# The input products of the feed-forwards as seven half-block products instead of eight

## The chip, the cores and the metric

The kernel runs on one core of a Trainium2 chip. The metric is the device time of one execution in microseconds (us). TensorE is called PE (its weight loads PEld), VectorE DVE, ScalarE ACT, GpSimd POOL; SP is the engine that issues most transfers. PSUM is the memory that PE writes.

## The reference, cut to what matters

Two transformer blocks in a row on 512 tokens of width D = 1024, all in float32. Three feed-forwards take part: two in the first block (before and after a mixer), one at the end of the second.

```python
def swiglu_ffn(h, w_in, w_out):              # DFF = 2816
    a, b = jnp.split(h @ w_in, 2, axis=-1)
    return (jax.nn.silu(a) * b) @ w_out

x = x + 0.5 * swiglu_ffn(rmsnorm(x, ffn1_norm_g), ffn1_w_in, ffn1_w_out)
...
x = x + 0.5 * swiglu_ffn(rmsnorm(x, ffn2_norm_g), ffn2_w_in, ffn2_w_out)
...
x = x + _swiglu(_rms(x, norm_ffn_w[l]), w_ffn_gate[l], w_ffn_up[l], w_ffn_down[l])
```

Between them stand the mixers (sparse attention, convolution, attention to a memory; then sliding-window attention and gated linear attention; then attention to a second memory), which the change leaves as they are.

## The kernel before, in words

Activations lie transposed: `X` is eight tiles of 128 features x 512 tokens. Every float32 operand of a product is split into a high part rounded to the matmul's type (a cast on ACT) and a low part (the rest, a subtraction on DVE or POOL); `mm3` (line 229) makes three matmuls of a product: high x high, high x low, low x high. `split` (258) does it for one tile.

`ffn` (513) works on 22 units c in three groups of 8, 7 and 7 (`FGROUPS`). A unit's weights are two tiles of 128 x 1024, one for the gate columns and one for the up columns, `f1_ab[2c]` and `[2c+1]`. `w` (272) loads one (`wr`, on SP) and splits it (`wh`, `wl`). `chunk` (302) multiplies it with the eight tiles `xh`, `xl` of the normalised X: 24 matmuls of 512 columns into one PSUM tile, so 48 for a unit. The row scale `rb` of the normalisation is applied after the product: z = gate * rb, Silu, * rb, u = z * up, and u is split. After the units of a group come its output products: eight chunks, one for each tile of X, each over the group's 8 or 7 u tiles, added to X. In the first unit (c = 0) the product walks over k for both tiles together, so that it can start before the last tile of X is normalised. `lag` (2 in the first feed-forward, else 1) says after which unit the row scale `rc`, `rb` is made; until then products wait in PSUM. The third feed-forward ends in `tail` (569), whose last four output tiles are made in halves of 256 columns.

`hook(n)` is called as each X tile is final; it begins the next stage's normalisation: `norm_x` (389) multiplies by the gain and splits (`xs`), `norm_sq` (378) sums squares (on POOL for the first stage). `project` (1249) is the last product of a mixer and calls it; so does the output loop of `xattn` (1662). In the first feed-forward, `tick` (507) lets small steps of other work in: the position tables (`tables`, 473: DMAs on POOL, a few matmuls) and the preparation of the memory (`mem_prep`, 643). The weights' low parts are made on DVE in the feed-forwards, and two thirds of them on POOL in the mixers (`wes`).

A scheduler lays the instructions on each engine's queue in advance, by program order as their inputs come ready; at run time each queue goes in that order. PSUM has eight tiles of 512: tags g (3), s (2), t (2), o (1); `psf` (222) goes round the first seven.

Of the kernel before, what the change touches and what calls it, by code (L numbers as in the profile page):

```python
# [14 lines left out]
P = 128  # L15
# [14 lines left out]
LINEW = 64  # L30

# [169 lines left out]
class _Net:  # L201
# [24 lines left out]
    def mm(self, o, l, r, first, last):  # L226
        self.pm = self.nc.tensor.matmul(o, l, r, start=first, stop=last)  # L227

    def mm3(self, o, lh, ll, rh, rl, first, last):
        self.mm(o, lh, rh, first, False)  # L230
        self.mm(o, lh, rl, False, False)
        self.mm(o, ll, rh, False, last)
# [22 lines left out]
    def copy(self, o, x):  # L255
        self.nc.scalar.copy(o, x)  # L256
# [116 lines left out]
    def begin_norm(self, key=None):  # L373
        self.nk = key
        self.acc = self.t(self.g, [P, S], F32, "acc", 1)
        self.xh, self.xl = [], []
# [12 lines left out]
    def norm_x(self, j):  # L389

        if self.nk:
            h = self.t(self.g, [P, S], F32R, "xs", 16)
            l = self.t(self.g, [P, S], F32R, "xs", 16)
            gc = self.cc(self.nk, j)
            self.last = self.nc.scalar.activation(h, self.X[j], AF.Copy, scale=gc)
            self.stt(l, self.X[j], gc, h.bitcast(F32), ALU.mult, ALU.subtract)
            self.xh.append(h)
            self.xl.append(l)
# [27 lines left out]
    def setup(self):  # L426
# [13 lines left out]
        for j in range(KT):  # L440
            nc.sync.dma_start(self.X[j], a["xT"][j])
            if j < 4:
                ws[j % 2][j // 2]()
# [29 lines left out]
    def tables(self, p):  # L473

        nc, a = self.nc, self.a
        box = {}

        def line(key, width, n):
            def go():
                if "rel" not in box:  # L480
                    box["rel"] = self.t(p, [33, 16], F32, "rel", 1)
                    nc.vector.memset(box["rel"], 1.0)
                    nc.gpsimd.dma_start(box["rel"][0:32], a["rel"])
                oh = self.load(key, pool=p)
                box[key] = self.t(p, [16, 2 * width], F32, key + "l", 1)
                for j in range(2):
                    ps = self.ps("t", (16, width))
                    s = slice(width * j, width * (j + 1))
                    self.mm(ps, box["rel"], oh[:, s], True, True)
                    nc.vector.tensor_copy(box[key][:, s], ps)  # L490
# [8 lines left out]
        def cmpline():  # L499
            nc.gpsimd.dma_start(self.drel, box["oh1"])  # L500
            nc.gpsimd.dma_start(self.dcmp, box["oh2"])

        st = [line("oh1", LINE // 2, 2), line("oh2", 512, 2), cmpline]
# [9 lines left out]
    def ffn(self, key, scale, hook, lag=1):  # L513
        nc = self.nc
        with self.pool(key) as p:
            self.wps = [self.wps[0], (p, D, 2)]
            for gi, (k0, k1) in enumerate(FGROUPS):
                uh, ul = [], []
                wait = []
                for c in range(k0, k1):  # L520
                    pa, pb = self.psf(), self.psf()
                    if c == 0:

                        ws = [self.w(key + "_ab", u, D) for u in range(2)]
                        for k in range(KT):
                            s = slice(k * P, (k + 1) * P)
                            for ps, (h, l) in zip((pa, pb), ws):
                                self.mm3(ps, h[:, s], l[:, s], self.xh[k], self.xl[k], k == 0, k == KT - 1)
                    else:
                        self.chunk(pa, key + "_ab", 2 * c, self.xh, self.xl)  # L530
                        if c == lag:
                            with self.tc.issue_after(self.pm.ins):
                                self.rc
                        self.chunk(pb, key + "_ab", 2 * c + 1, self.xh, self.xl)
                    if c == lag:
                        with self.tc.issue_after(self.pm.ins):
                            self.rb
                    wait.append((pa, pb))
                    if c < lag:
                        continue  # L540
                    for pa, pb in wait:
                        z = self.t(p, [P, S], F32, "z", 3)
                        self.mul(z, pa, self.rb)
                        self.act(z, z, AF.Silu)
                        self.mul(z, z, self.rb)
                        u = self.t(p, [P, S], F32, "u", 2)
                        self.mul(u, z, pb)
                        h = self.t(p, [P, S], F32R, "uh", 8)
                        l = self.t(p, [P, S], F32R, "ul", 8)
                        self.split(h, l, u)  # L550
                        uh.append(h)
                        ul.append(l)
                        self.tick()
                    wait = []
                last = gi == len(FGROUPS) - 1
                if last and hook is None:
                    self.tail(p, f"{key}_o{gi}", uh, ul)
                    break
                for n in range(KT):
# [4 lines left out]
                    if last:  # L564
                        hook(n)
# [1222 lines left out]
```

## Time and profile before

| | us |
|---|---|
| median of 3 runs (2480.50 to 2482.72) | 2481.11 |
| profiled execution | 2480.74 |
| its span | 2478.7 |
| PE busy | 2406.0 (97%) |
| DVE, ACT, POOL busy | 1433.1, 980.3, 407.7 |

The span runs from the first to the last instruction. The first feed-forward lies at about 7 to 380 us, the second at 1158 to 1518, the third at 2100 to the end. Matmuls overlap, so their pace is read from the distance of their starts, not from the duration of one.

### The profile page before, as it was taken

Reading aid. Unit: us, or ns where it says so; the run is one execution under the profiler, and the core shown is the slowest. Engines: PE = TensorE matmul, PEld = TensorE weight load, DVE = VectorE, ACT = ScalarE, POOL = GpSimd, SP = SyncE. Lnnn points to the kernel's source line nnn. Section 1 sums busy time; section 2 is a strip of 40 time slices with the busy share of each in tenths; the row PEclk is TensorE's granted clock in tenths of the full one; section 3 lists DMA queues with packets and bytes.
Section 4 is the critical chain, followed back from the end, with each engine's and each line's share of the span. In section 5 each row is a group of like instructions: output and inputs, shape, how many; then the busy total and the mean of one; then the engine's idle time right before and its main releaser. Section 6 shows DMA issues by size and latency. Waiting matters only on the chain.

```text
span 2478.7 us, 30104 instructions
## 1 busy us (share of the span) xinstructions
PE 2406.0 (97%) x11566; PEld 1990.4 (80%) x11566; DVE 1433.1 (58%) x2594; ACT 980.3 (40%) x1743; POOL 407.7 (16%) x223
## 2 busy tenths in 40 slices
PE   9999999999999999999999999999999998999998
PEld 6888888787777887778888888787788886888887
DVE  7444455864777666775534444558765277644444
ACT  4222234343444544453322233544565256322222
POOL 5000004231222232231000002121212430000000
PEclk9999999999999999999999999999999999999999
DMA  5622325221222121124232322121212242322321
GB/s 196 187 93 96 99 88 172 96 101 54 78 69 76 53 87 69 65 87 134 95 101 86 108 87 98 59 94 54 68 69 76 99 145 68 124 94 92 104 80 49
DMA packets 84051, 232.26 MB, mean 94 GB/s; under 512 B 16305, under 2 KB 25457, under 8 KB 83908
## 3 DMA queue, kind: packets, MB, share of 16 engines
q1 hardware_dynamic: 75460, 224.87, 27.3%
q0 software_dynamic: 8448, 5.48, 0.7%
q8 instruction: 91, 1.49, 0.2%
q14 instruction: 52, 0.43, 0.1%
HBM read 223.85 MB, written 11.64 MB: 95 GB/s over the span
## 4 chain that ended last, share of the span: by engine, by line
PE 47%; DVE 5%; ACT 1%; issue 1%; POOL 0%; DVEq 0%; ACTq 0%; POOLq 0%
PE g L227 24%; PE s L227 11%; PE t L227 10%; PE o L227 1%; PE t L235 1%; DVE q L238 0%; DVE sp L1523 0%; DVE wl L238 0%; DVE xs L250 0%; DVE og L238 0%; DVE ptl L238 0%; ACT wh L256 0%; DVE og L250 0%; DVE x L238 0%; DVE stl L238 0%
## 5 line engine op out<-in xcount | busy, mean ns | idle before, releaser
L227 PE MATMUL g<-xs,wh 128*128 128x512 f32 x2800 | 892.2, 396 | 1.3 <-DVE kcr L238 1.0
L256 ACT CAST wh<-wr 128x1024 fp32r<-128x1024 f32 (+6 forms) x405 | 411.5, 1017 | 1046.9 <-PE g L227 400.4
L227 PEld LDWEIGHTS g<-xs,wh 128*128 128x128 f32 x2800 | 523.1, 190 | 106.3 <-issue 4.1
L227 PE MATMUL g<-xs,wl 128*128 128x512 f32 x1400 | 553.2, 395 | 1.5 <-DVE wl L238 1.5
L238 POOL TENSOR_TENSOR wl<-wr,wh 128x1024 fp32r<-128x1024 f32 (+6 forms) x134 | 309.9, 2314 | 1415.7 <-ACT wh L256 1366.7
L238 DVE TENSOR_TENSOR wl<-wr,wh 128x1024 fp32r<-128x1024 f32 (+4 forms) x271 | 335.5, 1240 | 78.4 <-ACT wh L256 72.6
L227 PEld LDWEIGHTS g<-xs,wl 128*128 128x128 f32 x1400 | 265.3, 190 | 59.3 <-issue 3.1
L227 PE MATMUL t<-xs,wh 128*128 128x512 f32 x672 | 208.8, 392 | 2.1 <-ACT xs L256 1.9
L227 PE MATMUL s<-xs,wh 128*128 128x512 f32 x672 | 208.2, 390 | 2.0 <-ACT wh L256 1.8
L227 PEld LDWEIGHTS s<-xs,wh 128*128 128x128 f32 x672 | 126.1, 188 | 31.9 <-ACT wh L256 3.4
L227 PEld LDWEIGHTS t<-xs,wh 128*128 128x128 f32 x672 | 126.6, 189 | 29.1 <-ACT xs L256 2.3
L227 PE MATMUL t<-xs,wl 128*128 128x512 f32 x336 | 131.6, 392 | 0.3 <-DVE wl L238 0.3
L227 PE MATMUL s<-xs,wl 128*128 128x512 f32 x336 | 130.9, 390 | 0.0
L253 ACT ACTIVATE sp<-sp,nm 128x128 f32<-128x128 f32 x192 | 101.9, 532 | 48.9 <-DVE nm L1071 37.8
L238 DVE TENSOR_TENSOR ptl<-t,pth 128x512 fp32r<-128x512 f32 (+1 forms) x128 | 72.9, 603 | 56.8 <-ACT pth L256 56.5
L256 ACT CAST pth<-t 128x512 fp32r<-128x512 f32 (+1 forms) x128 | 61.7, 520 | 98.4 <-PE t L235 98.2
L227 PE MATMUL g<-uh,wh 128*128 128x512 f32 (+1 forms) x242 | 92.1, 380 | 0.0
L227 PE MATMUL g<-uh,wl 128*128 128x512 f32 (+1 forms) x242 | 92.0, 380 | 0.0
L227 PE MATMUL g<-ul,wh 128*128 128x512 f32 (+1 forms) x242 | 92.0, 380 | 0.0
L227 PEld LDWEIGHTS t<-xs,wl 128*128 128x128 f32 x336 | 63.5, 189 | 14.1 <-DVE wl L238 0.8
L227 PEld LDWEIGHTS s<-xs,wl 128*128 128x128 f32 x336 | 63.1, 188 | 12.9
L238 POOL TENSOR_TENSOR y<-y,rmb 128x512 f32<-128x512 f32 x2 | 3.6, 1786 | 402.8 <-ACT rmb L256 402.8
(468 smaller groups left out, 3947.8 us busy)
## 6 DMA issues: line engine op xcount, KB each, us to landing
wr<-f_ab SPq DMA_DIRECT2D x130, 512.0 KB, 3.5
wr<-f_o SPq DMA_DIRECT2D x48, 448.0 KB, 3.2
wr<-m_f SPq DMA_DIRECT2D x40, 512.0 KB, 3.2
wr<-m_o SPq DMA_DIRECT2D x40, 512.0 KB, 3.4
wr<-f_o SPq DMA_DIRECT2D x24, 512.0 KB, 3.6
wr<-m_q SPq DMA_DIRECT2D x12, 512.0 KB, 3.5
dline<-drel POOLq DMA_DIRECT2D x8, 640.0 KB, 20.1
wr<-m_km SPq DMA_DIRECT2D x8, 512.0 KB, 3.6
```

The costliest lines, as they stand in the source:

```text
L227: self.pm = self.nc.tensor.matmul(o, l, r, start=first, stop=last)
L235: self.nc.tensor.transpose(o, i, self.ident)
L238: (e or self.nc.vector).tensor_tensor(o, x, y, op=op)
L253: return self.nc.scalar.activation(o, x, f, **k)
L256: self.nc.scalar.copy(o, x)
```

## The change

A unit's product is seen as blocks. Rows: gate, up. Inner dimension: the first and the second half of the 1024 features. Columns: the first and the second 256 tokens (H = 256). With a11, a12 the halves of the gate weights and a21, a22 those of the up weights, and likewise x1 and x2 (tiles 0 to 3 and 4 to 7 of X) cut into lo and hi, the four result blocks come from seven block products and sums (Winograd's form of Strassen's algorithm). A block product is 4 k-tiles x 3 matmuls of 256 columns. For each unit `wforms` makes four sums of weight halves on POOL and seven splits; for each feed-forward `form_x` makes, in place of `norm_x`, the four sums of X halves for each pair of tiles (n, n+4) and splits all seven 256-column blocks (`bh`, `bl`). Tiles of X are taken in the order 0, 4, 1, 5, 2, 6, 3, 7. The first two units of the first feed-forward stay plain. A unit's last block (a22) is put behind the first block of the next unit. The memory's preparation moves into the last group of the first feed-forward; the steps of `tables` each take their own tiles and issue their own transfer.

```diff
+    def form_x(self, n):
+        i = n % 4
+        xg = self.t(self.tp, [P, S], F32, "xg", 3)
+        self.last = self.act(xg, self.X[n], AF.Copy, scale=self.cc(self.nk, n))
+        self.half_x[n] = xg
+        if self.B[i] is None:
+            self.B[i] = [self.t(self.fp, [P, 64 + 7 * H], F32R, k, 4)[:, 48:48 + 7 * H] for k in ("bh", "bl")]
+        bh, bl = self.B[i]
+        def parts(c, x):
+            n = x.shape[-1]
+            self.last = self.copy(bh[:, c:c + n], x)
+            self.tt(bl[:, c:c + n], x, bh[:, c:c + n].bitcast(F32), ALU.subtract)
+        if n < 4:
+            parts(0, xg[:, :H])
+        else:
+            parts(H, xg)
+        if i in self.half_x and i + 4 in self.half_x:
+            x1, x2 = self.half_x[i], self.half_x[i + 4]
+            t = self.t(self.tp, [P, 4 * H], F32, "xt", 1)
+            t1, t2, t3, t4 = (t[:, k * H:(k + 1) * H] for k in range(4))
+            self.tt(t1, x1[:, H:], x1[:, :H], ALU.subtract)
+            self.tt(t2, x2[:, H:], t1, ALU.subtract)
+            self.tt(t3, x2[:, H:], x1[:, H:], ALU.subtract)
+            self.tt(t4, x2[:, :H], t2, ALU.subtract)
+            parts(3 * H, t)
...
+    def wforms(self, arr, c):
...
+        (a11, a12), (a21, a22) = ((r[:, :B], r[:, B:]) for r in raw)
+        s1, s2, s4, s3 = (self.t(self.fw, [P, B], F32, "ws", 4) for _ in range(4))
+        e = nc.gpsimd
+        self.tt(s1, a21, a22, ALU.add, e)
+        self.tt(s2, s1, a11, ALU.subtract, e)
+        self.tt(s4, a12, s2, ALU.subtract, e)
+        self.tt(s3, a11, a21, ALU.subtract, e)
...
+            for m, (k, x) in enumerate(pair):
+                out[k] = h[:, m * B:m * B + B], l[:, m * B:m * B + B]
+                self.split(*out[k], x)
...
+        def first():
+            box["w"] = self.wforms(key + "_ab", c)
+            box["r1"] = self.psf(half)
+            self.block(box["r1"], box["w"]["a11"], 0, True)
+        def second():
+            w = box["w"]
+            e1 = box["e1"] = self.t(p, [P, H], F32, "e1", 2)
+            self.copy(e1, box["r1"])
+            r5 = box["r5"] = self.psf(half)
+            self.block(r5, w["s1"], 3, True)
+            e5 = box["e5"] = self.t(p, [P, H], F32, "e5", 2)
+            self.copy(e5, r5)
+        def rest():
...
+            self.block(r2, w["s2"], 4, True)
+            self.block(r1, w["a12"], 1)
+            self.tt(r2, r2, e1, ALU.add)
+            self.copy(e2, r2)
+            self.block(r5, w["s4"], 2)
+            self.block(r2, w["s3"], 5)
+        def last():
+            e3 = box["e3"] = self.t(p, [P, H], F32, "e3", 2)
+            self.copy(e3, box["r2"])
+            self.block(box["r2"], box["w"]["a22"], 6)
+        def act(uh, ul):
+            e = nc.gpsimd
+            lo, hi = slice(0, H), slice(H, S)
+            z = self.t(p, [P, S], F32, "z", 2)
+            self.mul(z[:, lo], box["r1"], self.rb[:, lo])
+            self.tt(z[:, hi], box["r5"], box["e2"], ALU.add)
+            self.mul(z[:, hi], z[:, hi], self.rb[:, hi], e)
+            self.act(z, z, AF.Silu)
+            self.mul(z, z, self.rb, e)
+            c22 = box["e5"]
+            self.tt(c22, c22, box["e3"], ALU.add, e)
+            u = self.t(p, [P, S], F32, "u", 1)
+            self.mul(u[:, lo], z[:, lo], box["r2"])
+            self.mul(u[:, hi], z[:, hi], c22, e)
+            self.keep_u(u, uh, ul)
...
+            for c in range(n + 1):
...
+                if c < np_:
+                    waiting.append(self.plain(p, key, c, *parts[gi]))
+                    continue
+                if c < n:
+                    first, second, rest, end, act = self.unit(p, key, c)
+                    first()
...
+                if prev:
+                    prev[0]()
+                if c < n:
+                    second()
...
+                if prev:
+                    waiting.append(prev[1])
+                if c >= lag:
+                    flush()
+                if c and gi != group[c - 1]:
+                    products(group[c - 1])
+                if c < n:
+                    rest()
+                    prev = end, lambda act=act, gi=gi: act(*parts[gi])
...
-                    self.norm_x(n)
+                    (self.form_x if key.startswith("ffn") else self.norm_x)(n)
```

## Rows read from the trace of the kernel before

**Rows 1.** The page: busy us by engine, share of the span, instructions.
```profile
PE 2406.0 (97%) x11566; PEld 1990.4 (80%) x11566; DVE 1433.1 (58%) x2594; ACT 980.3 (40%) x1743; POOL 407.7 (16%) x223
```

**Rows 2.** Chain of waits in the second feed-forward: start us, us, what.
```profile
1186.73 5.44 PE s L227 x24
```

**Rows 3.** Busy time of the engines by stretch.
```profile
core 0: us, PE busy (x) PEld busy (x) DVE busy (x) ACT busy (x) POOL busy (x), PEclk, DMA share, GB/s
12.00:30.00 18.00, 17.42 (x74) 13.22 (x73) 17.96 (x11) 8.33 (x11) 17.84 (x11) 1.00 0.78 269
1168.00:1246.00 78.00, 78.00 (x354) 64.85 (x353) 39.36 (x58) 25.47 (x33) 0.00 (x0) 1.00 0.31 101
1246.00:1284.00 38.00, 38.00 (x169) 31.50 (x168) 14.01 (x15) 7.89 (x8) 0.00 (x0) 1.00 0.30 97
```

**Rows 4.** PE in order of time, output products in halves, third feed-forward.
```profile
2443.31 0.28 PE L227 MATMUL t<-uh,wh 128*128 128x256 f32 x1
...
2445.82 0.28 PE L227 MATMUL g<-uh,wh 128*128 128x256 f32 x1
```

**Rows 5.** Groups by form: xcount, busy us, mean ns (second: tile kr, min/median/max ns).
```profile
L238 DVE TENSOR_TENSOR ul<-u,uh 128x512 fp32r<-128x512 f32 x66 | 44.9, 683 | 0.0
L238 DVE TENSOR_TENSOR kr<-g,rmb x8: 401/424/426, 383.5 to 402.8; 128x256 f32<-128x256 f32 x8
...
L256 ACT CAST wh<-wr 128x1024 fp32r<-128x1024 f32 x327 | 343.4, 1052 | 826.9 <-PE g L227 312.8 <-issue 260.4 <-PE s L227 128.4
L253 ACT ACTIVATE z<-z 128x512 f32<-128x512 f32 x66 | 41.1, 627 | 0.9 <-DVE z L238 0.8
L256 ACT CAST uh<-u 128x512 fp32r<-128x512 f32 x66 | 40.5, 616 | 2.9 <-DVE u L238 2.9
L395 ACT ACTIVATE xs<-x,cols 128x512 fp32r<-128x512 f32 x48 | 33.1, 718 | 17.4 <-DVE x L250 14.0 <-DVE x L238 2.5 <-DMA cols<-cols 0.8
L256 ACT CAST pth<-t 128x256 fp32r<-128x256 f32 x32 | 11.6, 364 | 0.0
...
L238 POOL TENSOR_TENSOR x<-x,ga 128x512 f32<-128x512 f32 x8 | 10.3, 1288 | 31.8 <-DVE ga L250 31.8
L496 POOL DMA_DIRECT2D dline<-drel x8 | 8.6, 1071 | 35.4 <-issue 33.7 <-DMA drel<-oh1l 1.7
L238 POOL TENSOR_TENSOR wl<-wr,wh 128x256 fp32r<-128x256 f32 x1 | 0.8, 772 | 3.4 <-DMA wr<-cw 3.4
```

**Rows 6.** DVE and POOL in order of time: start us, us, instruction.
```profile
10.18 1.23 DVE L250 SCALAR_TENSOR_TENSOR xs<-x,cols,xs 128x512 fp32r<-128x512 f32 x1 [0.48 <-ACT xs L395]
10.82 1.74 POOL L238 TENSOR_TENSOR wl<-wr,wh 128x512 fp32r<-128x512 f32 x1
11.51 1.60 DVE L250 SCALAR_TENSOR_TENSOR xs<-x,cols,xs 128x512 fp32r<-128x512 f32 x1
...
17.82 12.72 DVE L238 TENSOR_TENSOR wl<-wr,wh 128x1024 fp32r<-128x1024 f32 x6
```

**Rows 7.** PE in order of time, first feed-forward: unit 2 begins; row scale.
```profile
30.75 0.61 PE L227 MATMUL s<-xs,wh 128*128 128x512 f32 x2
...
37.73 0.27 PE L227 MATMUL o<-ones,acc 128*128 128x2 f32 x1 [1.39 <-POOL acc L238]
```

**Rows 8.** In order of time, start of the second feed-forward.
```profile
1157.52 0.62 PE L227 MATMUL g<-xs,wh 128*128 128x512 f32 x2
...
1158.24 0.68 DVE L250 SCALAR_TENSOR_TENSOR x<-t,x 128x512 f32<-128x512 f32 x1
```

**Rows 9.** In order of time, start of the third feed-forward.
```profile
2095.75 0.69 DVE L238 TENSOR_TENSOR x<-s,x 128x512 f32<-128x512 f32 x1 [1.02 <-PE s L227]
...
2097.55 0.74 DVE L250 SCALAR_TENSOR_TENSOR xs<-x,cols,xs 128x512 fp32r<-128x512 f32 x1
...
2100.31 0.39 PE L227 MATMUL g<-xs,wh 128*128 128x512 f32 x1
...
2103.92 1.22 DVE L238 TENSOR_TENSOR wl<-wr,wh 128x1024 fp32r<-128x1024 f32 x1
```

More of the change, by code (lines that the diff above doesn't have):

```diff
@@ L224, in psf, with mm, mm3 @@
         return self.ps("gsgtgst"[self.pi], shape)
[L226 to L232, printed above, removed]
+    def mm(self, o, l, r, first, last, more=False):
+        self.pm = self.nc.tensor.matmul(o, l, r, start=first, stop=last, skip_group_check=more)
+    def mm3(self, o, lh, ll, rh, rl, first, last, more=False):
+        self.mm(o, lh, rh, first, False, more)
+        self.mm(o, lh, rl, False, False, more)
+        self.mm(o, ll, rh, False, last, more)
     def tr(self, o, i):
@@ L255, in copy @@
     def copy(self, o, x):
-        self.nc.scalar.copy(o, x)
+        return self.nc.scalar.copy(o, x)
     def split(self, h, l, x):
@@ L439, in setup @@
         ws = [self.w("f1_ab", u, D, split=True) for u in range(2)]
-        for j in range(KT):
+        for n, j in enumerate(ORDER):
             nc.sync.dma_start(self.X[j], a["xT"][j])
-            if j < 4:
-                ws[j % 2][j // 2]()
+            if n < 4:
+                ws[n % 2][n // 2]()
         for u in range(2):
@@ new lines, in block, with unit @@
+    def block(self, ps, w, b, first=False):
+        h, l = w
+        c = slice(b * H, b * H + H)
+        for i in range(4):
+            s = slice(i * P, i * P + P)
+            bh, bl = self.B[i]
+            self.mm3(ps, h[:, s], l[:, s], bh[:, c], bl[:, c], first and i == 0, i == 3, not first)
+    def unit(self, p, key, c):
+        nc = self.nc
+        box = {}
+        half = (P, H)
+        def first():
[11 more added lines that the diff above has]
+        def rest():
+            w, r1, r5, e1 = (box[k] for k in ("w", "r1", "r5", "e1"))
+            e2 = box["e2"] = self.t(p, [P, H], F32, "e2", 2)
+            r2 = box["r2"] = self.psf(half)
+            self.block(r2, w["s2"], 4, True)
[23 more added lines that the diff above has]
+            self.keep_u(u, uh, ul)
+        return first, second, rest, last, act
@@ new lines, in keep_u, with plain, act @@
+    def keep_u(self, u, uh, ul):
+        h = self.t(self.up, [P, S], F32R, "xs", 16)
+        l = self.t(self.up, [P, S], F32R, "xs", 16)
+        self.split(h, l, u)
+        uh.append(h)
+        ul.append(l)
+        self.tick()
+    def plain(self, p, key, c, uh, ul):
+        pa, pb = self.psf(), self.psf()
+        if c == 0:
+            ws = [self.w(key + "_ab", u, D) for u in range(2)]
+            for k in ORDER:
+                s = slice(k * P, (k + 1) * P)
+                for ps, (h, l) in zip((pa, pb), ws):
+                    self.mm3(ps, h[:, s], l[:, s], self.xh[k], self.xl[k], k == 0, k == KT - 1)
+        else:
+            self.chunk(pa, key + "_ab", 2 * c, self.xh, self.xl)
+            self.chunk(pb, key + "_ab", 2 * c + 1, self.xh, self.xl)
+        def act():
+            z = self.t(p, [P, S], F32, "z", 2)
+            self.mul(z, pa, self.rb)
+            self.act(z, z, AF.Silu)
+            self.mul(z, z, self.rb)
+            u = self.t(p, [P, S], F32, "u", 1)
+            self.mul(u, z, pb)
+            self.keep_u(u, uh, ul)
+        return act
@@ L515, in ffn @@
+    def ffn(self, key, scale, hook, np_=0, lag=1, after=None):
         with self.pool(key) as p:
             self.wps = [self.wps[0], (p, D, 2)]
[L517 to L554, printed above, removed]
@@ L555, in ffn, with flush, products @@
+            self.fw = p
+            parts = [([], []) for _ in FGROUPS]
+            group = [gi for gi, (k0, k1) in enumerate(FGROUPS) for _ in range(k0, k1)]
+            waiting = []
+            def flush():
+                while waiting:
+                    waiting.pop(0)()
+            prev = None
+            def products(gi):
+                k0, k1 = FGROUPS[gi]
+                uh, ul = parts[gi]
                 last = gi == len(FGROUPS) - 1
+                if last:
+                    after()
@@ L556, in ffn @@
                 if last and hook is None:
                     self.tail(p, f"{key}_o{gi}", uh, ul)
-                    break
-                for n in range(KT):
+                    return
+                for n in ORDER:
                     po = self.psf()
@@ L1259, in project @@
         hook = self.hook
-        for n in range(KT):
+        for n in ORDER:
             po = self.psf()
@@ L1712, in step, with after @@
                 return hook
+            fin = None
+            def after():
+                self.fpool.__exit__(None, None, None)
+                if self.fpool is not fin:
+                    self.open_x()
             def done(tag):
```

155 lines of the change are left out of this document (109 added, 46 removed).

## The prediction

> **What bounds the kernel now.** I read the page first: TensorE (PE) is busy for 97% of the span [rows 1]. That number hides which stages have slack, so next comes the chain of waits inside the second feed-forward: it is PE alone, 5.44 us for each run of 24 matmuls, a run on the heels of the other; one of them stands in [rows 2]. The table of stretches shows it at the full clock (1.00), and room on the others: in the 78 us of input products DVE works 39 us, ACT 25 us, POOL nothing; in the 38 us of output products DVE works 14 us [rows 3]. So a feed-forward is bound by the count and pace of matmuls, and 50% of DVE and all of POOL stand free. The profiled execution took 2480.74 us, against a median of 2481.11; the sum below is made against 2480.7.
>
> **What the change removes.** A unit (one block of 128 gate and 128 up columns) has 48 matmuls of 512 columns now: two runs of 24, 10.88 us [rows 2]. It becomes 84 matmuls of 256 columns. The kernel already has such a stream, in its last output products: from 2443.31 to 2445.82 twenty-one of them start, 0.120 us apart [rows 4], against 0.227 us for 512 (5.44/24). Half the columns cost 53%, not 50%, so seven eighths of the work costs 84 x 0.120 = 10.08 us: 0.80 us less a unit. Two units of the first feed-forward stay plain; 64 units change: **-51 us**. The Trainium skill ("TensorE: Matmul & The Clock Gate", Back-to-back issue gap) gives N/2.4 + 2.5 ns, an estimate of 109 and 216 ns; by that a unit would lose 1.2 us and the whole 76 us. The rows are this kernel's own operand type, so they decide.
>
> **What it adds per unit.** ACT: seven casts of 512 at 0.62, four copies of 256 from PSUM at 0.36, Silu and the cast of u: 7.0 us. DVE: seven low-part subtractions and that of u, 8 x 0.68, and four operations of 256 with a PSUM operand at 0.42: 7.1 us. POOL: four weight sums and one product of 512 at 1.29, three operations of 256 at 0.77: 8.8 us [rows 5]. Each alone fits under 10.08 us.
>
> DVE and POOL do not add up that way. At 10.18 us a DVE subtraction and a POOL one meet: POOL starts at 10.82 and ends 1.15 us after the DVE one (11.41 to 12.56), and the next DVE one, begun at 11.51, ends 0.55 us after POOL's (13.11) [rows 6]; alone they take 1.29 and 0.74 [rows 5, 9]. So an operation of DVE with two SBUF operands and one of POOL take turns, 1.70 us a pair of 512. From 12 to 30 us both read as 99% busy [rows 3], and six of DVE's 1024-wide splits take 12.72 us, 2.1 each instead of 1.22 [rows 6]: each mostly waits for the other. In turns, a unit needs POOL 5 x 1.15 + 3 x 0.63 (0.77 less the same 0.14) and DVE 8 x 0.55: **12.0 us** of the shared path, more than PE's 10.08. The operations with one PSUM operand are not counted: the eight of 256 at 383 to 403 us, where POOL splits weights too, spread from 0.40 to 0.43 us only [rows 5]. The Trainium skill ("SBUF — State Buffer", Who interferes with whom) speaks against this change: the shared port pair is an exclusive lock, and the second to issue fully blocks until the first finishes. By whole durations that would be 8.8 + 5.4 = 14.2 us a unit; the trace agrees on the turns, but shows 1.70 us for a pair where whole durations give 1.97.
>
> What softens it is the output products. In those 38 to 43 us DVE has 14 us of work and POOL none [rows 3], so the next unit's four sums (4.6 us) and its first two splits (1.1) can be done ahead; the single set of four sum tiles and five split buffers allow no more. Between two such stretches PE has seven units, 70.6 us, and some 4 us more before the last u tile is read (18 matmuls at 0.227). The shared path needs 7 x 12.0 less what is done ahead and what the next stretch takes over (three sums, five splits: 6.2), about 72 us. That fits, just. The first eight units have no such stretch before them: 8 x 12.0, less unit 0's sums (4.6) and with unit 8's first sum and splits (2.3), 94 us against 83.5 of PE (eight units, two blocks of the ninth) and the same 4. So the stall lies between nothing (PE's bound) and 64 x 1.96 = 125 us (turns without any catching up). I take 6.5 us for each first group and 2 us for the hand-offs in each of the others, 33 us for three feed-forwards with f1's shorter first group counted alike: units of 10.6 us on average. What is late next is DVE: behind a subtraction that waits for POOL stands the addition of e1 to r2, for which ACT's copy e2 waits and PE's block s3 with it; two blocks (2.9 us) cover it, so it breaks only where two POOL operations fall into that time. In the same way the copy e3 is covered by the next unit's first block (1.44 us).
>
> **The starts.** The forms cost DVE, per pair of X tiles, a subtraction of 256, one of 512, four differences of 256 and a subtraction of 1024: 0.42 + 0.68 + 1.68 + 1.22 = 4.0 us, against two of 0.74 for the plain split [rows 9], and nearly all of them must be there before the second block of the first unit.
> - f1: PE leaves the two plain units at 30.75 us and so far waits first near 36 us, 1.39 us for POOL's sum of squares [rows 7]; DVE and POOL have no free time before [rows 3]. DVE is rid of four of the six splits [rows 6] and gets 16 us of forms. They begin in earnest when the splits of unit 1 are through, at 17.82 + 2 x 2.12 = 22 us; POOL squares X until 37.7, and there DVE's work takes 1.7 times as long (12.72 against 6 x 1.22). By 37.7 us 9 of the 16 us are done, by 45 all; with the pieces fitted in before 22 us I say 43. PE waits 12 us; bounds 7 (no turns: 22 + 16 - 30.75) and 18 (all of it at the slow pace).
> - f2: the last product ends near 1157.5 us and X is added at 1158.24 [rows 8]. That takes 0.69, then a scaled copy 0.72, differences 1.7, cast 1.05, subtraction 1.22 [rows 5, 9]: 5.4 us, of which the first block and three quarters of the second cover 2.5. Now the product walks over k and covers 9.5 us. With one or two sums of POOL in between: 5 us; bounds 3 and 8.
> - f3: the products before it are short: PE is through at 2100.31 us, DVE begins with X at 2095.75 [rows 9]. Two additions and a pair of forms are 5.4 us, four pairs 21.5 us: 2117.3. Less the same 2.5 us PE waits 14 us; bounds 8 (if half is overlapped) and 20.
> Sum **+31 us**, bounds 18 and 46.
>
> **The rest.** The last unit's u follows its products by z, Silu, two steps on POOL and a split, some 5 us against 4.1 of cover: 1 us for each feed-forward, 3 us. The eight table transfers that POOL issues in f1 take 1.07 us each [rows 5], and now stand in one queue with the sums: half of it counts, 4 us. The memory's preparation moves from f1's start to its last eight products, where DVE is idle most of the time [rows 3]; its ten steps are hidden there, but for its last row sums, whose cover is three products of the next stage. The order of X, the loads on SP (the same weights, 512 KB a tile) and the right-hand pools move nothing that PE waits for.
>
> **Sum:** 2480.7 - 51 + 33 + 31 + 3 + 4 = 2500.7, **2501 us**. This is the likeliest case, with a chance of 0.50; its own range is 2477 to 2530 (stalls of 20 to 50 us, starts of 20 to 43).
>
> **Rivals.**
> - *PE stays the bound* (0.34): the output products give DVE and POOL enough to catch up, and most turns fall where nobody waits. For it: the 72 against 74.6 us above; ACT at 70%, PSUM with seven buffers for three in use. Against it: the first groups, and the starts, which no output product precedes. Stalls 8, starts 22, rest 3: 2480.7 - 51 + 33 = 2463 us; with bare starts (18) and no stall 2450. This is the other side of my forecast, and it decides at units of about 10.3 us: below that the -51 outweighs the starts.
> - *The turns bind all the time* (0.16): the order of the queues, laid out in advance, keeps POOL from running ahead, as its steps for u wait for PE and Silu and the sums after them wait along. Every unit takes 12.0 us: +74 us, and with starts and rest (38) 2593 us; if a third is caught up, about 2551. For it: the stretch at 12 to 30 us does not get ahead until its work ends. Against it: the free stretches every 7 units.
> The Trainium skill's lock ("SBUF — State Buffer", Who interferes with whom) is this rival's rule; with its 14.2 us a unit, an estimate, it would add 64 x 3.3 = 212 us.
>
> **Chances.** A measurement of this kernel can tell about 0.2% (5 us) from no change. Of the first case 0.02 lies below 2476 and 0.10 within 5 us, of the second 0.02 within; so faster 0.34, same 0.12, slower 0.54. The range of 2452 to 2555 leaves out the bare end of the second case and most of the third, 0.2 together.
>
> **What would show it.** Right: 256-column blocks 0.120 us apart; units of 10.3 to 11.2 us, PE idle behind DVE's splits (wl) or the sums more in the later units of a group than in the first; subtractions of DVE beside POOL at 1.2 to 1.7 us; PE idle for about 12 us near 31 us, and some 14 us at the start of the third feed-forward. The forecast is wrong if the units run at 10.1 us, if a pair of turns is not 1.70 us for the sums, or if the forms are hidden at the starts.

## The result, and the profile after

The changed kernel took **2740.28 us** (median of 4 runs, 2736.55 to 2745.01) against 2480.81 of the kernel before beside it: ratio **1.1048, 95% interval [1.1027, 1.107]**. Forecast were 2501 us and a range of 2452 to 2555. The direction was right, the size was not: +256 us in the profiled execution (span 2734.8 against 2478.7) instead of +20.

The page answers to [rows 1]. PE's busy time grew although it has an eighth less of these products to do, and POOL's is two and a half times its former one:

```profile
PE 2448.6 (90%) x13870; PEld 2112.8 (77%) x13870; DVE 1776.9 (65%) x3047; ACT 1196.3 (44%) x2363; POOL 1052.2 (38%) x736
```

To see where the time went I cut the span at the Silus of the gate (22 in a feed-forward, one for each unit; the output products of a group fall between Silu 7 and 8 and between 14 and 15). Us of each stretch, from the starts of these instructions in the profiled executions:

| stretch | before | after | e1 | e3 | e5 | e17 |
|---|---|---|---|---|---|---|
| start to f1's Silu 0 | 50.0 | 68.4 | 67.9 | 60.3 | 65.7 | 56.6 |
| f1, Silu 0 to 7 | 51.4 | 90.9 | 91.0 | 77.7 | 57.5 | 52.8 |
| f1, Silu 7 to 21 | 234.8 | 273.2 | 262.4 | 221.1 | 219.9 | 223.2 |
| to f2's Silu 0 | 847.0 | 855.8 | 858.4 | 843.8 | 853.7 | 856.1 |
| f2, Silu 0 to 7 | 58.8 | 88.0 | 84.1 | 62.4 | 63.3 | 58.3 |
| f2, Silu 7 to 21 | 233.9 | 269.5 | 259.8 | 222.1 | 217.8 | 220.8 |
| to f3's Silu 0 | 651.3 | 680.9 | 678.9 | 668.4 | 673.0 | 672.0 |
| f3, Silu 0 to 7 | 58.7 | 81.7 | 79.9 | 59.6 | 63.1 | 59.1 |
| f3, Silu 7 to 21 | 233.9 | 269.6 | 257.6 | 221.7 | 217.5 | 218.4 |
| to the end | 58.9 | 56.9 | 55.9 | 55.5 | 54.9 | 54.8 |

Read the stretches of Silu 7 to 21 first: 14 units with two sets of output products, 36 to 38 us longer each, 2.6 us a unit: 13.5 us on average, where [rows 2] gives 10.88 and the forecast had 10.6. Within a group a steady unit takes 14.3 us; the last one or two of a group take 11.1 to 13.2. Over 62 units (14 in the later groups of each feed-forward, 20 in the three first groups) that is 162 us. The starts and the first groups make the other 94.

The view of busy time by stretch, in f3's second group (columns as in [rows 3], whose middle line it answers to):

```profile
2464.00:2547.00 83.00, 65.57 (x499) 62.71 (x498) 56.75 (x72) 35.68 (x76) 55.08 (x46) 0.94 0.19 68
```

PE, then full, now works 66 of 83 us, and DVE 57, and POOL 55; neither is full by its busy time. So the waits come next. PE's, over the whole span (waited for: us in total, times, longest):

```profile
PE g L230 <- ACT e L259: 63.4, 47, 4.6
PE s L230 <- ACT e L259: 55.8, 37, 5.7
PE t L230 <- ACT e L259: 33.3, 29, 2.3
PE o L230 <- ACT rsh L259: 20.0, 7, 5.0
```

PE waits 152 us for ACT's copies e, of which I had said that blocks cover them. One unit in order of time shows why they are late, first PE (start, us, [idle before <- releaser]):

```profile
2489.49 0.28 PE L230 MATMUL s<-bh,wh 128*128 128x256 f32 x1
...
2490.74 0.28 PE L230 MATMUL s<-bh,wl 128*128 128x256 f32 x1
2493.26 0.58 PE L230 MATMUL g<-bh,wh 128*128 128x256 f32 x1 [2.25 <-ACT e L259]
2493.64 0.42 PE L230 MATMUL g<-bl,wh 128*128 128x256 f32 x1
2493.86 0.42 PE L230 MATMUL g<-bh,wl 128*128 128x256 f32 x1
```

then ACT, whose queue has Silu and two casts ahead of the copy e3 (the one that ends at 2493.20):

```profile
2491.28 0.63 ACT L256 ACTIVATE z<-z 128x512 f32<-128x512 f32 x1 [2.81 <-POOL z L241]
2491.82 1.12 ACT L259 CAST wh<-ws 128x512 fp32r<-128x512 f32 x2
2492.84 0.36 ACT L259 COPY e<-g 128x256 f32<-128x256 f32 x1
```

then DVE, up to a unit later:

```profile
2496.29 0.42 DVE L241 TENSOR_TENSOR u<-z,g 128x256 f32<-128x256 f32 x1 [1.88 <-POOL e L241]
...
2501.74 0.67 DVE L241 TENSOR_TENSOR wl<-ws,wh 128x512 fp32r<-128x512 f32 x1
...
2502.78 1.60 DVE L241 TENSOR_TENSOR wl<-wr,wh 128x512 fp32r<-128x512 f32 x1
2504.30 0.41 DVE L241 TENSOR_TENSOR z<-g,e 128x256 f32<-128x256 f32 x1
```

and POOL beside it:

```profile
2496.19 1.29 POOL L241 TENSOR_TENSOR ws<-wr,wr 128x512 f32<-128x512 f32 x1
...
2502.55 1.28 POOL L241 TENSOR_TENSOR ws<-ws,wr 128x512 f32<-128x512 f32 x1 [2.22 <-issue]
2504.79 0.73 POOL L241 TENSOR_TENSOR z<-z,rb 128x256 f32<-128x256 f32 x1 [0.96 <-DVE z L241]
```

This is a loop. DVE's subtraction begins 0.23 us after a sum of POOL, lasts 1.60 us instead of 0.68 and ends 0.55 us after it; z waits behind it on DVE, POOL's product and ACT's Silu wait for z, e3 stands behind Silu, and PE's block a22 waits for e3. Five blocks later PE gives DVE the next z. POOL itself stands 2.22 us ahead of that sum. The profile names no releaser, but the sum is written into one of the single set of four tiles, and in the steady units of this kernel, e1, e4 and e8 it begins 0.13 us after DVE's subtraction of a sum (`wl<-ws`, here the one that ends at 2502.41): it waits for its tile. So two causes were to be told apart: the **order of ACT's queue**, and the **turns** of DVE and POOL.

The granted clock comes on top. Behind this wait it is 0.50, so 1.2 of 2.4 GHz, and matmuls are 0.21 us apart; then it is full again, and it stays full behind the next unit's wait, which is as long (busy time by stretch):

```profile
2493.30:2496.20 2.90, 2.90 (x13) 2.90 (x14) 1.11 (x2) 0.36 (x2) 2.31 (x3) 0.50 0.00 0
2496.60:2501.00 4.40, 4.40 (x41) 4.40 (x41) 4.26 (x5) 2.49 (x6) 3.73 (x3) 1.00 0.00 2
2507.50:2510.40 2.90, 2.87 (x25) 2.87 (x26) 2.24 (x5) 1.39 (x3) 2.27 (x3) 1.00 0.00 0
```

That next wait, in PE's order of time:

```profile
2507.53 0.39 PE L230 MATMUL t<-bh,wh 128*128 128x256 f32 x1 [2.25 <-ACT e L259]
2507.75 0.28 PE L230 MATMUL t<-bl,wh 128*128 128x256 f32 x1
2507.87 0.28 PE L230 MATMUL t<-bh,wl 128*128 128x256 f32 x1
```

Added up over the second group of f3, a unit is 9.6 us of blocks at the full clock, some 1 us more on average for those at the half, and some 3.5 us of idle time.

### The profile page after: what moved, and what is told of

Same layout as the page of the kernel before. It is cut to its first block, busy times and chain, and to the rows that moved or that the text cites. A ratio compares the mean times of both kernels' runs of the same rounds, so it can differ in the third digit from the quotient of the medians.

```text
span 2734.8 us, 36622 instructions
## 1 busy us (share of the span) xinstructions
PE 2448.6 (90%) x13870; PEld 2112.8 (77%) x13870; DVE 1776.9 (65%) x3047; ACT 1196.3 (44%) x2363; POOL 1052.2 (38%) x736
## 5 line engine op out<-in xcount | busy, mean ns | idle before, releaser
L230 PE MATMUL g<-xs,wh 128*128 128x512 f32 (+1 forms) x2434 | 775.2, 396 | 6.7 <-ACT wh L259 4.6
L259 ACT CAST wh<-wr 128x512 fp32r<-128x512 f32 (+5 forms) x469 | 395.4, 845 | 561.1 <-PE g L230 239.8
L241 POOL TENSOR_TENSOR wl<-wr,wh 128x1024 fp32r<-128x1024 f32 (+6 forms) x134 | 310.8, 2321 | 847.3 <-ACT wh L259 814.6
L230 PE MATMUL g<-xs,wl 128*128 128x512 f32 (+1 forms) x1217 | 480.0, 394 | 5.4 <-DVE wl L241 2.8
L241 DVE TENSOR_TENSOR wl<-wr,wh 128x512 fp32r<-128x512 f32 (+5 forms) x335 | 384.0, 1148 | 54.7 <-ACT wh L259 49.8
L241 DVE TENSOR_TENSOR wl<-ws,wh 128x512 fp32r<-128x512 f32 x256 | 244.0, 971 | 115.0 <-ACT wh L259 109.6
L230 PE MATMUL g<-bh,wh 128*128 128x256 f32 x756 | 229.0, 303 | 70.9 <-ACT e L259 63.4
L230 PEld LDWEIGHTS g<-xs,wl 128*128 128x128 f32 x1217 | 231.6, 190 | 55.9 <-DVE wl L241 4.3
L230 PE MATMUL g<-bl,wh 128*128 128x256 f32 x756 | 223.9, 296 | 2.0 <-DVE bl L241 2.0
L230 PE MATMUL g<-bh,wl 128*128 128x256 f32 x756 | 223.8, 296 | 1.8 <-DVE wl L241 1.8
L230 PE MATMUL s<-bh,wh 128*128 128x256 f32 x500 | 151.0, 302 | 55.9 <-ACT e L259 55.8
L230 PE MATMUL t<-bh,wh 128*128 128x256 f32 x536 | 162.0, 302 | 39.0 <-ACT e L259 33.3
L230 PE MATMUL t<-bl,wh 128*128 128x256 f32 x536 | 157.9, 295 | 0.9 <-DVE bl L241 0.9
```

What stands on the lines that cost most here:

```text
L241: (e or self.nc.vector).tensor_tensor(o, x, y, op=op)
L259: return self.nc.scalar.copy(o, x)
```

## The experiments

**e1, the order alone.** `box["c3"]` is the copy e3:
```
-            self.act(z, z, AF.Silu)
+            with self.tc.issue_after(box["c3"].ins):
+                self.act(z, z, AF.Silu)
```


> One edge in ACT's queue: the Silu of a unit is issued after the same unit's copy e3. Everything is still computed. Queue theory (PE waits 2.4 us a unit because e3 stands in ACT's queue behind Silu, which waits for DVE and POOL, and then runs 1.0 us more at the half clock): the wait of PE for e3 and the half-clock blocks go, units fall from 14.27 to 10.9-11.5 us, the kernel to 2520-2560 us. Turns theory (DVE's two-SBUF-operand work and POOL's take turns, and that path is 91% full in a steady unit): the wait moves to another tile, units stay at 13.0 us or more, the kernel at 2655 us or more.


Measured 2698.02 us, ratio 1.0877 [1.0851, 1.0903]; units 13.3 us. The order is worth 1.0 us a unit and 42 us in all; 13.3 us stay, as the turns theory said. What fills them can be counted from the starts and ends of the instructions, over four units of f2's second group. In e1 DVE or POOL is at work at every moment, 13.3 of 13.3 us. The path that they share (POOL, or a DVE operation without a PSUM operand) is in use for 12.7 us; in the other 0.6 us DVE works on an operand in PSUM and POOL waits. In the changed kernel the same count gives 12.7 us, 0.7 us, and 0.8 us in which neither works: this last part is what e1 takes away. One engine's idle time lies in the other's work. Busy time of e1 over the four units (a record holds also the time in which its operation stands for the other engine), then DVE and POOL in order of time:

```profile
1431.70:1485.10 53.40, 43.19 (x338) 40.81 (x338) 39.90 (x49) 24.97 (x52) 40.00 (x33) 0.97 0.24 78
...
1448.67 0.42 DVE L241 TENSOR_TENSOR u<-z,g 128x256 f32<-128x256 f32 x1 [3.13 <-POOL z L241]
1454.92 1.29 POOL L241 TENSOR_TENSOR ws<-ws,wr 128x512 f32<-128x512 f32 x1 [2.21 <-issue]
```

POOL's 2.21 us are the wait for its tile again. More sum tiles were not tried; as the shared path alone is in use for 12.7 us a unit, they could not bring e1 under that.

**e2 and e3, without the sums.** Both leave out the four weight sums, so they do not compute the product. In `wforms`, for e2 alone and for e3 together with e1's edit:
```
-        self.tt(s1, a21, a22, ALU.add, e)
...
-        self.tt(s3, a11, a21, ALU.subtract, e)
+        s1, s2, s4, s3 = a21, a12, a11, a22
```


> Left out: the four weight sums that POOL makes for a unit; raw halves are split in their place, so ACT, DVE and PE have the same instructions. ACT's queue still has Silu ahead of e3. Queue theory: only the DVE subtraction that stands in the loop gets shorter (1.60 to 0.68 us) and the loop with it: units 13.0-13.4 us, kernel near 2670. Turns theory: the shared path loses 4 x 1.15 us or more, units fall to 9.6-10.5 us (PE's bound), kernel 2430-2500.

> Both edits: no weight sums on POOL (left out, raw halves in their place), and Silu issued after e3. Either theory: nothing of the loop and little of the shared path is left, units at PE's own 9.6-10 us, kernel 2430-2470; what remains over 2481 less 64 x 1.3 us is the starts. If it stays over 2500, a third cause holds PE.


e2: 2532.12 us, 1.021 [1.0176, 1.0243], units 10.4 us. e3: 2494.66 us, 1.0062 [1.0042, 1.0083], units 9.9 us. POOL's sums cost 208 us of the 260, as the turns theory has it, and the units fell into its range; the order is 0.5 us a unit more. Both kernels lie above the 2500 and 2470 us that were expected at most. e3 shows why: PE's own pace for a unit is 9.9 us (forecast 10.08), and with units at that pace the kernel is still 17 us over the one before. The starts and the first groups, f1's above all (77.7 us for 51.4), eat all of the seventh product's 64 x 0.98 = 63 us.

**e4 and e8, POOL with the sums only.** e4 in `act`, e8 with e1's edit too:
```
         def act(uh, ul):
-            e = nc.gpsimd
+            e = nc.vector
```


> POOL's four steps for u (z hi times rb, z times rb, e5 plus e3, u hi) go to DVE; POOL keeps the four sums. Everything is still computed. ACT's queue still has Silu ahead of e3. Queue theory: the loop loses POOL's step and its hand-off (0.8 us) but puts it on DVE behind its splits: units 13-14.3 us, kernel 2660-2740. Turns theory: the shared path falls from 13 to about 4 x 1.15 + 10 x 0.55 = 10.1 us a unit, units 10.1-11 us, kernel 2470-2530.

> e4 (POOL's steps for u on DVE, sums on POOL) with Silu issued after e3 as in e1. Everything is still computed. Turns theory: in e4 DVE never rests (9.1 us of its own and some 0.97 us of waiting for each of four sums), so the order of ACT's queue is worth nothing there: units stay at 13.0 us, kernel 2645-2660. Queue theory: units lose another 1.0 us as from the changed kernel to e1, 12.0 us, kernel near 2590.


e4: 2655.1 us, 1.0706 [1.0674, 1.0737], units 13.0 us. e8: 2629.96 us, 1.0583 [1.0552, 1.0614], units 12.35 us. e4 came out beside the queue theory's numbers (13 us, 2660), far from the turns theory's 2470 to 2530, and e8 between the two. The turns theory's sum for e4 was wrong: it counted ten DVE operations at 0.55 us and left out that all sixteen of them stand in one queue. In e4 DVE stood some 0.7 us before the product of z, waiting for Silu, and that is what e8 gains. In e8 DVE hardly rests: 12.25 of 12.35 us a unit lie in its records. In order of time, DVE:

```profile
2428.36 1.60 DVE L241 TENSOR_TENSOR wl<-wr,wh 128x512 fp32r<-128x512 f32 x1
2429.88 0.41 DVE L241 TENSOR_TENSOR z<-s,e 128x256 f32<-128x256 f32 x1
2430.33 0.43 DVE L241 TENSOR_TENSOR z<-z,rb 128x256 f32<-128x256 f32 x1
2430.67 1.29 DVE L241 TENSOR_TENSOR wl<-ws,wh 128x512 fp32r<-128x512 f32 x2
2431.88 1.52 DVE L241 TENSOR_TENSOR e<-e,e 128x256 f32<-128x256 f32 x1
2433.32 1.79 DVE L241 TENSOR_TENSOR z<-z,rb 128x512 f32<-128x512 f32 x1
```

and POOL:

```profile
2428.12 1.29 POOL L241 TENSOR_TENSOR ws<-ws,wr 128x512 f32<-128x512 f32 x1 [2.22 <-issue]
2431.50 1.61 POOL L241 TENSOR_TENSOR ws<-wr,ws 128x512 f32<-128x512 f32 x1 [2.09 <-DVE wl L241]
2433.07 1.48 POOL L241 TENSOR_TENSOR ws<-wr,wr 128x512 f32<-128x512 f32 x1
```

Two subtractions in a row that start ahead of a sum take 1.29 us together; the addition of e, 256 wide, takes 1.52 us behind a sum and 0.42 without one (in e5). It ends at 2433.40, POOL's sum 1.15 us later, and DVE's product 0.56 us after that. POOL is busy half of the time at most here, and waits for nobody's z: it is not the length of its queue that binds, but that DVE stands while POOL works. DVE's own work is 9 x 0.60 + 7 x 0.34 = 7.8 us (the pace is read in e5, next), and each of four sums adds 1.14.

**e5, POOL silent.** e1, and `e = nc.vector` in `act` and in `wforms`.


> Silu after e3 as in e1, and POOL does nothing in a unit: its four sums and its four steps for u are DVE's. Everything is still computed. Turns theory: with POOL silent every DVE operation takes its own time, 12 subtractions and sums of 512 at 0.68, the rb product 0.69, four operations with PSUM at 0.42 and three of 256 at 0.43: 11.8 us a unit, and DVE is the bound; units 11.8-12.2 us, 1.2 us under e1 although DVE has eight more operations; kernel near 2600. Rival (DVE's long subtractions have another cause, ACT or the loads): DVE's 9.9 us of records a unit gets 4.7 us more work, units 14 us or more, kernel above 2740.


Measured 2486.53 us, 1.0019 [1.0007, 1.003]: **212 us less than e1, by moving eight operations a unit onto the fuller engine.** The rival, over 2740, is out. The time is lower than the 2600 expected, because DVE's operations start every 0.60 us (512) and 0.34 us (256), not every 0.68 and 0.42 as their durations say. In order of time:

```profile
2385.64 0.68 DVE L241 TENSOR_TENSOR xs<-u,xs 128x512 fp32r<-128x512 f32 x1
2386.24 0.69 DVE L241 TENSOR_TENSOR wl<-wr,wh 128x512 fp32r<-128x512 f32 x1
2386.84 0.42 DVE L241 TENSOR_TENSOR s<-s,e 128x256 f32<-128x256 f32 x1
2387.18 1.28 DVE L241 TENSOR_TENSOR wl<-ws,wh 128x512 fp32r<-128x512 f32 x2
...
2395.80 0.69 DVE L241 TENSOR_TENSOR xs<-u,xs 128x512 fp32r<-128x512 f32 x1
```

From one xs to the next are 10.16 us: 13 x 0.60 + 7 x 0.34 = 10.2. The same groups of DVE's instructions by form, in the changed kernel (busy us, mean ns, idle time before them):

```profile
L241 DVE TENSOR_TENSOR wl<-ws,wh 128x512 fp32r<-128x512 f32 x256 | 244.0, 971 | 115.0 <-ACT wh L259 109.6 <-issue 4.0
L241 DVE TENSOR_TENSOR wl<-wr,wh 128x512 fp32r<-128x512 f32 x194 | 208.1, 1074 | 4.2 <-ACT wh L259 1.6
```

and in e5:

```profile
L241 DVE TENSOR_TENSOR wl<-ws,wh 128x512 fp32r<-128x512 f32 x256 | 167.2, 688 | 7.2 <-ACT wh L259 7.2
L241 DVE TENSOR_TENSOR wl<-wr,wh 128x512 fp32r<-128x512 f32 x194 | 130.6, 688 | 0.1
```

**e6 and e7, the first feed-forward's order**, both on e1. e6 takes `self.tick()` out of `keep_u`; e7 writes the forms behind the plain units (`if forms and c == np_: forms()` in `ffn`).


> e1, and the steps of the tables and of the memory are taken only at output products, not at units (everything is still computed). In the first feed-forward the Silus come 23 us apart once, with DVE standing 8 us at its copy of a table row whose matmul PE reaches late. If that is what makes the first group irregular, f1 loses 10-20 us: kernel 2678-2688. If the first group is only late by the work that DVE and POOL are behind with from the start, the time moves by less than 5 us.

> e1, and in the first feed-forward the forms of X are written after the two plain units instead of before them (everything is still computed). If the order makes f1 start late (forms ahead of unit 1's weight splits in DVE's queue, PE idle from 28 to 40 us inside the plain products), PE does its plain products earlier and f1 gains 8-12 us: kernel 2686-2690. If DVE and POOL are simply full until 60 us, the idle time moves behind the plain products and the time stays within 4 us of e1's.


e6: 2711.56 us, 1.0911 [1.088, 1.0943]. The first group falls from 91.0 to 70.0 us, but Silu 7 to 21 grows from 262 to 296: the gain is given back, and 13 us with it, which neither branch had foreseen. e7: 2696.03 us, 1.0849 [1.0801, 1.0896], as e1: the order of the forms does not count where DVE is full.

**e9, POOL silent at the start too**, on e5:
```
-            return [lambda: load(slice(0, n // 2), e), lambda: load(slice(n // 2, n), nc.gpsimd), h, l]
+            return [lambda: load(slice(0, n // 2), e), lambda: load(slice(n // 2, n), e), h, l]
...
-                self.norm_sq(j, nc.gpsimd)
+                self.norm_sq(j)
```


> e5 (all of a unit's work on DVE, Silu after e3), and POOL is silent at the start of the first feed-forward too: ACT squares X, DVE adds the squares, DVE makes all the weight splits. Everything is still computed. In e5 the eighth Silu of f1 is 22 us later than in the kernel before. Turns theory: at f1's start POOL holds DVE off as in the units, so f1 gains 8 us or more although DVE has 7 additions and two half splits more: kernel 2470-2479. Rival (DVE is full there with its own work, 16 us of forms): the added 7 us of work cost as much as POOL's silence gives, kernel within 4 us of e5's 2486.5.


Measured 2476.67 us, 0.9975 [0.9966, 0.9984]. Silu 0 of f1 comes at 56.7 us, 9 us sooner than in e5, as expected.

**The cross-attention: e10, e11, e13, e14, e18.** e10 and e11 open `xo` and `xa` ahead of `open_u`; e10 was to stand on e5, but has e9's edit in it as well, so it is e11's kernel a second time. e13 (on e9), e14 (on the changed kernel) and e18 (e13 with two buffers) open them there too, and prepare the memory inside the projection:
```
+        if between:
+            between()
         self.reload()
...
+        self.project("m2_mo", 0.5, kv)
```


> e5, and the buffers of the memory's keys and values for the cross-attention are opened before the projection that ends the second mixer, as the kernel before has it, not after it. Everything is still computed. If the 12 us that the cross-attention came later in the changed kernel are that order, the kernel goes to 2473-2477. If its preparation is late for another reason (DVE's or POOL's queue), it stays within 3 us of e5's 2486.5.

> e9 and e10 together; everything is still computed. If both hold, the gains add: 2460-2468, faster than the kernel before by 0.5% or more. If the starts are bound by the forms, 2480 or more.

> e9 (a unit's work all on DVE, POOL silent at the start of f1), and the memory of the cross-attention is prepared in the middle of the projection before it (after the split of M, before the products; single buffers for the raw memory, which the SBUF leaves room for), as the kernel before does it in effect. Everything is still computed. If the 15 us by which the cross-attention comes later than before (offset -14.4 us ahead of the projection's end, +1 behind it, in the run named both) are this preparation's place, the kernel gains 8-14 us on e9: 2463-2469. If they are the forms or the row sums, it stays within 3 us of 2477.

> The changed kernel with this one edit alone (memory of the cross-attention prepared in the middle of the projection). Everything is still computed. If the place of the preparation is the cause, the stretch from the last Silu of f2 to the first of f3 falls from 681 us by 8-14 us, kernel 2726-2732; if not, 2737-2743.

> e13 with two buffers for the raw memory again (its squares go through the ring of the row sums' squares). Everything is still computed. If e13 lost 10 us because the single buffers make the memory's loads, squares and casts run one behind the other, the stretch from f2's last Silu to f3's first falls from 683.6 to 660-668 us and the kernel to 2462-2470. If PE's place for the products of the memory is what holds it, the stretch stays at 675 us or more and the kernel above 2475.


e10 2480.59 us, 0.9998 [0.9986, 1.001]; e11 2478.93 us, 0.9992 [0.9983, 1.0001]; e13 2487.85 us, 1.0022 [1.0011, 1.0033]; e14 2749.95 us, 1.1091 [1.1066, 1.1115]; e18 2478.62 us, 0.9984 [0.9974, 0.9993]. None beat e9 (e14: the changed kernel), so the explanation fell in all five. e13 and e14 move waits of PE from the cross-attention into the projection (to f3's Silu 0: 683.6 and 689.3 us, e9 673.4, the changed kernel 680.9), e18 takes that back with the second buffer (672.0) and gains nothing. In the changed kernel the last product of the cross-attention comes 633.8 us behind f2's last Silu, before 624.3. Why it comes those 9.5 us later stays open.

**e12, e16, e17, one factor later.** e17 on e9, e12 on e11, e16 on e12 with e13's edit:
```
-            self.mul(z, z, self.rb, e)
+            if not late:
+                self.mul(z, z, self.rb, e)
...
+                    y = self.t(p, [P, S], F32, "z", 2)
+                    self.mul(y, po, self.rb)
+                    self.stt(self.X[n], y, scale, self.X[n], ALU.mult, ALU.add)
```


> e11, and the second factor rb of a unit is put on the output products (24 products of 512 with PSUM a feed-forward, in the stretch where DVE has time) instead of on z (0.60 us of DVE a unit); the last group of f3 keeps it on z. The same sums, in another order. DVE-bound theory (units of 10.2 us are DVE's 12 x 0.60 and the rest): a unit's DVE work falls to 9.6 us, under PE's 9.9 of the run without sums; units 9.9, 50 x 0.3 = 15 us less than e11. If units of 10.2 us are bound by the order of queues, nothing is gained (within 4 us).

> e12 (e9, the pools of the run named both, and rb of a unit put on the output products) with the memory prepared early as in e13. Everything is still computed. If the gains add: 2462-2468, 0.5-0.8% under the kernel before. If PE's own work at the lower clock fills what is saved, 2473-2478.

> e9 with the rb of a unit put on the output products, and nothing moved in the cross-attention. Everything is still computed. In e12 the same edit stood beside the moved pools, which cost 2 to 4 us by themselves: so e12's 2477.9 less 2 to 4, 2472-2476. DVE-bound theory of the 10.2 us units, by the three first groups of e12 (14 us less than in e11, of which later groups gave 8 back): 2470-2474. If DVE was not the bound, 2475-2479 as e9.


e12 2477.9 us, 0.9982 [0.9971, 0.9993]; e16 2483.55 us, 1.0011 [0.9998, 1.0024]; e17 **2472.81 us, 0.9962 [0.995, 0.9973]**. e12 is 1 us under e11, within what was named as no gain; e16 lies above both its ranges; e17 lies in the range of the DVE-bound theory, but its interval overlaps e9's, so that it is faster than e9 is not shown. By stretches the theory is half right. In e17 nearly all units behind the first groups run at 9.9 us, PE's own pace, and its first groups are 5.0, 5.0 and 3.7 us shorter than e9's (57.8, 63.3, 62.8): that fits DVE as the bound of the 10.2 us there. But Silu 7 to 21 takes 4.1, 3.3 and 0.6 us longer than in e9 (219.1, 217.5, 217.8), with the factor now at the output products. e17 has the lowest time, 0.4% under the kernel before: the seven products pay, a little, once POOL does none of their work.

## Why the prediction was wrong

- *The seventh product, -51 us.* Right, a little low: the 12 matmuls of a block are 0.114 us apart (2489.49 to 2490.74 above, eleven steps), not 0.120; e3's units of 9.9 us give -63.
- *"1.70 us a pair of 512", "12.0 us of the shared path".* The pair was right: in e8's rows above POOL's sum ends 1.15 us after the DVE operation ahead of it and DVE's next 0.56 after the sum, 1.71, and a sum adds 1.14 to a unit there. The path was a little low: counted, it is in use for 12.7 us. **The step that failed first is to take the path for the whole unit, wherever the turns bind.** A unit takes 14.3 us: 12.7 of the path, 0.7 in which DVE works on an operand in PSUM while POOL waits for it, and 0.8 in which neither works, which e1's order takes away. The rule of the Trainium skill ("SBUF — State Buffer", Who interferes with whom), that a DVE instruction with two SBUF inputs contends with a GpSimd one that reads SBUF and that the lock is exclusive, holds here: beside a sum DVE's 0.68 us become 1.60. The 14.2 us that whole durations give come close to the unit's 14.3 by luck: the path they are the sum for is 12.7. That operations with one PSUM operand stay out of it held too: the product at 2496.29 above takes its 0.42 us beside a sum begun at 2496.19. But they are not free, as they stand in DVE's queue.
- *"What softens it is the output products", "10.6 us on average".* **The second failure of the same step:** seven units less 11.9 us of lead were to fit into 74.6 us, for which I took 2 us of stall. (With 6.5 us for three first groups and 2 us for six others the stall is 31.5 us, not the 33 of the sum.) Seven units at 14.3 us exceed seven at PE's 9.9 by 31 us; the later groups of f2 are 24 us longer than e3's, so a stretch gives back some 7 us, not 11.9. DVE and POOL do the four sums there, as said, and then stand, and the units behind the stretch take 14.3 us again. The unit's price weighs more: with 12.0 us a unit and 7 us given back a group would have been 77 us, against 74.6; with 14.3 and 11.9 it is 88. Busy time of the changed kernel in such a stretch, which answers to the last line of [rows 3]:

```profile
1384.00:1422.00 38.00, 38.00 (x170) 31.44 (x169) 13.88 (x15) 7.46 (x8) 6.86 (x4) 1.00 0.30 106
```

  POOL's four operations are the sums, and DVE is idle for 24 of the 38 us. In f2's second group the Silus stand 14.3 us apart five times and 13.2 once. So the second rival was the mechanism, "the turns bind all the time". I gave it 0.16 and 12.0 us a unit. Its reason, that the order laid out in advance keeps POOL from running ahead, fits with POOL's waits for z, for Silu and for a free sum tile, but no run took it alone.
- *"The copy e3 is covered by the next unit's first block."* Wrong: some 2.2 us of wait in each steady unit, as e3 stands in ACT's queue behind a Silu that needs DVE and POOL. I costed the cover of PE's work and did not look at what is queued ahead on ACT. Worth 42 us with the sums (e1), 37 without (e2 to e3).
- *Starts, +31 us.* To the first Silus it is 18 + 9 + 30 = 57 us. The first groups take another 24, 11 and 5 us beyond their units' share, where the forecast had 6.5 each under the stalls; with the 2 us that the end gains, this is, but for rounding, the 94 above. f1: its first Silu comes 18 us later, its first changed unit 23 us later (at 53.3 us; unit 2 began at 30.75 before), where 12 were forecast and 18 was the bound. DVE is full and POOL nearly so from 12 to 60 us, 15 us longer than I counted (busy time):

```profile
12.00:60.00 48.00, 33.30 (x145) 26.24 (x144) 47.97 (x48) 22.38 (x37) 40.11 (x25) 0.82 0.29 101
```

  and PE waits inside the plain units for their own weight splits:

```profile
35.31 0.72 PE L230 MATMUL g<-xs,wh 128*128 128x512 f32 x1 [4.63 <-ACT wh L259]
40.63 0.80 PE L230 MATMUL t<-xs,wl 128*128 128x512 f32 x1 [4.61 <-DVE wl L241]
```

  f2: first Silu +9, forecast 5 and at most 8. f3: +30 before its first Silu, of which 9.5 up to the end of the cross-attention, so 20 against 14, at the bound. There the row scale is late, whose steps alternate with weight splits on DVE from 2313 to 2321 us:

```profile
2321.70 0.33 PE L230 MATMUL o<-identr,rsh 128*128 128x128 f32 x1 [2.54 <-ACT rsh L259]
```

- *"The right-hand pools move nothing that PE waits for."* Not refuted: opening them earlier (e11) gained nothing. The 9.5 us of the cross-attention stand in no term of the forecast.
- *The rest.* The last stretch gained 2 us instead of losing. What the table transfers cost cannot be told apart from f1's first group.
- *The side.* The forecast had slower as the likelier side, and slower it was, but by units that it took for an unlikely case. Even e3, which has neither sums nor their turns, is slower than before; "PE stays the bound" at 2463 us was approached only by e17 (2472.8), with Silu behind e3, POOL silent and one factor moved.

The whole by these terms: -63 for the product, +222 for what units take over 9.9 us (62 x 3.58), +94 for starts, first groups and the cross-attention: 253 of the 256. The 94 are what the units leave over, so the sum is no proof of them.

## What to carry to other kernels

An operation on POOL with SBUF operands is not free room beside a DVE with such operands: in e8 a sum of 512 on POOL added 1.14 us to DVE's unit, and the same sum on DVE takes 0.60 (e5). Add that price to the start-to-start times of all that stands in DVE's queue, and compare with the bound before giving POOL anything; what the two wait for each other comes on top. Then follow each in-order queue once round: a copy that frees PE's next block must not stand behind an activation that waits for two other engines. And a free stretch counts for catching up only as far as there are buffers, and an order of instructions, that let work be done ahead in it.

## What the runs showed that I had not expected

Moving eight operations from POOL to a DVE that was already busier made the kernel 212 us faster. A DVE operation of 512 that meets a POOL one shows 1.6 us in the profile and ends 0.55 us after POOL's; alone it shows 0.68 and the next begins after 0.60, so durations in a row of DVE operations overstate by some 0.08 us each. The half clock explains little: PE's granted clock fell to 0.50 behind one wait of 2.25 us and stayed at 1.00 behind the next of the same length. In e1's second group of f3 it is full, and the units there take 13.3 us as in f2's second group, where it falls to 0.50 twice. Busy time of e1 in f3's second group:

```profile
2464.00:2547.00 83.00, 71.82 (x477) 64.42 (x477) 51.20 (x62) 32.64 (x63) 42.60 (x35) 1.00 0.26 86
```

How much of the 1.0 us that e1 gained a unit is the order by itself and how much the half clock in the changed kernel's loop, the runs do not separate.
